# One 512-column matmul into a spare bank in the first up group, in place of six ahead of gate groups

## The chip, the core and the metric

The kernel runs on one core of a Trainium2 chip. The metric is the time of one execution on the device in microseconds, as the median of several runs; a profiled execution gives the rows shown here. The engines are named as in the profile: PE is TensorE's matmul row and PEld its weight loads, DVE is VectorE, ACT is ScalarE, POOL is GpSimd, and SP issues most of the DMAs.

## What is computed

One layer of an encoder on 256 positions of width 2048, in float32. Cut to what matters:

```
proj = rmsnorm(x, norm1_gain) @ w_in            # queries, keys and values of two groups of heads
o_d  = differential attention, 4 heads;  o_l = dilated windows, 8 heads
x    = x + concat(o_d, o_l) @ w_out
g, u = split(rmsnorm(x, norm2_gain) @ w_gate_up)  # 2 x 5632 columns
g    = depthwise_conv(g, conv_w, conv_b)          # width 3, over positions
x    = x + (silu(g) * u) @ w_down
out  = rmsnorm(x, final_gain)
```

## The kernel before

Each weight matrix is read from memory once, as 196 raw tiles of 128 x 2048 floats. Half a tile is a *unit*, and there are 392 of them, worked through in a fixed order that is written out by hand as a list (`add_unit`): 32 units for the values, 64 for queries and keys, 32 for the output projection, 176 for gate and up, 88 for the down projection.

To get near float32 accuracy, weights and activations are split into a high and a low part (`split`): ACT rounds a copy to the high part (line 121), and DVE subtracts it from the source to get the low part (line 122). A product is then three matmuls: high x high, high x low and low x high. `split_unit` does this for a unit three slots ahead of its use.

`products` (line 212) issues a unit's matmuls, all through `mm` (line 210 in the profile). There are two forms. In form A (values, output and down projection) a block of activations is the stationary operand and the weights move past it, 512 columns at a time; 12 matmuls make a unit. In form B (queries and keys, gate and up) a 128 x 128 block of weights is stationary and 256 positions of the activations move; 24 matmuls make a unit: eight on the high weights with the high activations, eight on the high weights with the low activations, eight on the low weights. In the profile the first 16 read whi and the last 8 read wlo.

In the gate and up stage there are 22 pairs. A pair is a gate group and then an up group, each of four units over k tiles 0-3, 4-7, 8-11 and 12-15, so 96 matmuls in a group and 192 in a pair. All four units of a group add into one accumulator of two banks (`acc`, two of them in turn). When a group is done, `gate` and `silu` or `gated` empty it on DVE and ACT. The pool `pat` has four more banks, handed out by `at_tile` (line 62): for scores, transposes, the broadcast of the token scale (line 150) just ahead of the first up group, and the last quarter of the down projection.

After the unit's own bookkeeping, and only in form B, a condition in `products` (line 236) picks out some units in which one more matmul is issued ahead of the 24. It takes the unit's first block of high weights as stationary operand, moves both parts of one k tile of the activations, 2 x 256 = 512 columns, and writes a bank of `pat` that nothing reads. Before the change the condition holds for the first unit of the gate groups of pairs 1, 5, 9, 13, 17 and 21:

```
            if U["first"] and U["key"][0] == "g" and U["key"][1] % 4 == 1:
                mm(at_tile(), wh[:, 0, :128], a[:, U["kts"][0]], True, True)
```

The order of instructions on every engine is that of the program (a manual schedule): the loop at the end loads raw tiles on SP's queue, splits the unit three slots ahead, issues the products of the present unit, and then the work that `at_slot` has put behind it.

Of the kernel before, what the change touches and what calls it, by code (L numbers as in the profile page):

```python
# [49 lines left out]
def encoder_layer(ctx, tc, xT_d, x_d, w_d, sm_d, tab_d, fg_d, id_d, oh_d, lnc_d, out_d):  # L50
# [11 lines left out]
    def at_tile():  # L62
        return pat.tile([128, 512], F32, name="at", tag="at")
# [145 lines left out]
    def mm(out, lhsT, rhs, start, stop):  # L209
        nc.tensor.matmul(out, lhsT, rhs, start=start, stop=stop)  # L210

    def products(s, ts=(0, 1)):
        U = units[s]
        if U["first"]:
            if U["key"] == ("d", 3):
                accs[U["key"]] = [at_tile(), at_tile()]
            else:
                P = acc.tile([128, 2, 512], F32, name="acc", tag="acc")
                accs[U["key"]] = P if U["form"] == "B" else [P[:, 0], P[:, 1]]
        P = accs[U["key"]]  # L220
        a = A[U["act"]]()
        hi, lo = W[s]
        nk = len(U["kts"])
        if U["form"] == "A":
            wh, wl = (w.rearrange("p (k c) -> p k c", k=2) for w in (hi, lo))
            for i, t in ((i, t) for i in range(2) for t in ts):
                kt = U["kts"][i]
                st, sp = U["first"] and i == 0, U["last"] and i == 1
                ah = a[:, kt, 0, t * 128:(t + 1) * 128]
                al = a[:, kt, 1, t * 128:(t + 1) * 128]  # L230
                mm(P[t], ah, wh[:, i], st, False)
                mm(P[t], ah, wl[:, i], False, False)
                mm(P[t], al, wh[:, i], False, sp)
        else:
            wh, wl = (w.rearrange("p (k c) -> p k c", k=4) for w in (hi, lo))
            if U["first"] and U["key"][0] == "g" and U["key"][1] % 4 == 1:

                mm(at_tile(), wh[:, 0, :128], a[:, U["kts"][0]], True, True)

            for j, (w, x_) in enumerate(((wh, 0), (wh, 1), (wl, 0))):  # L240
                for i, c in ((i, c) for i in range(nk) for c in range(2)):
                    mm(P[:, c, :S], w[:, i, c * 128:(c + 1) * 128], a[:, U["kts"][i], x_],
                       U["first"] and j == 0 and i == 0, U["last"] and j == 2 and i == nk - 1)
# [234 lines left out]
    for h in range(NH):  # L478
        g = 2 * h if h < 4 else h + 4
# [183 lines left out]
    for s in range(-AHEAD, NU):  # L663
        while n_loaded < NU // 2 and n_loaded * 2 <= s + AHEAD + 4:
            for _ in load_raw(n_loaded, 2 if n_loaded < 5 else 1):
                pass
            n_loaded += 1
            if X0 <= n_loaded < X0 + 4:
                load_x(n_loaded - X0)
        v = s + AHEAD  # L670
        if v < 8:
            split_unit(v, 2, lambda i: split_x(2 * v + i))
        elif v < NU:
            split_unit(v)
        if s == NU - AHEAD:
            break
        if s >= 0:
            products(s)
            del W[s]
            for f, a in post.pop(s, ()):  # L680
                f(*a)
    assert not post

    for t in range(2):
        for u in range(s, NU):
            products(u, (t,))
        final(t)
# [96 lines left out]
```

## Time and profile before

| what | value |
|---|---|
| median of 3 runs | 1137.55 us (1137.03 to 1138.54) |
| profiled execution, its own time | 1137.56 us |
| span of its instructions | 1135.8 us |
| TensorE matmul busy | 1123.0 us, 99% |
| TensorE weight load busy | 1043.9 us, 92% |
| VectorE busy | 677.6 us, 60% |
| ScalarE busy | 548.3 us, 48% |
| mean granted TensorE clock | 0.998 |

A row of the profile with two times gives the sum and the mean of one. Matmuls are pipelined, so the recorded duration of one is longer than the distance from its start to the next one's start. That distance is called the pitch here; it is taken from starts or from the length of a stretch by its count. The span is what lies between the first and the last instruction.

### The profile page before, as it was taken

Reading aid. Unit: us, or ns where it says so; the run is one execution under the profiler, and the core shown is the slowest. Engines: PE = TensorE matmul, PEld = TensorE weight load, DVE = VectorE, ACT = ScalarE, POOL = GpSimd, SP = SyncE. Lnnn points to the kernel's source line nnn. Section 1 sums busy time; section 2 is a strip of 40 time slices with the busy share of each in tenths; the row PEclk is TensorE's granted clock in tenths of the full one; section 3 lists DMA queues with packets and bytes.
Section 4 is the critical chain, followed back from the end, with each engine's and each line's share of the span. In section 5 each row is a group of like instructions: output and inputs, shape, how many; then the busy total and the mean of one; then the engine's idle time right before and its main releaser. Section 6 shows DMA issues by size and latency. Waiting matters only on the chain.

```text
span 1135.8 us, 18692 instructions
## 1 busy us (share of the span) xinstructions
PE 1123.0 (99%) x7930; PEld 1043.9 (92%) x7930; DVE 677.6 (60%) x841; ACT 548.3 (48%) x770; POOL 22.0 (2%) x40
## 2 busy tenths in 40 slices
PE   8999999999999999999999999999999999999996
PEld 6879999999988899999999999999999888888885
DVE  6844666766655575666666666656666545454543
ACT  7544456666555454544444454445444434343432
POOL 0000000001000000000000000000000000000000
PEclk9999999999999999999999999999999999999999
DMA  9568445445454546455555645454554655555552
GB/s 326 202 246 331 171 173 197 164 170 192 149 184 151 209 163 221 161 211 187 185 183 189 209 166 220 164 207 159 213 194 178 237 202 191 185 191 204 199 186 74
DMA packets 34092, 219.87 MB, mean 194 GB/s; under 512 B 3904, under 2 KB 4288, under 8 KB 9432
## 3 DMA queue, kind: packets, MB, share of 16 engines
q1 hardware_dynamic: 31536, 211.17, 52.0%
q0 software_dynamic: 1776, 6.69, 1.6%
q8 instruction: 62, 1.02, 0.3%
q10 hardware_dynamic: 696, 0.81, 0.2%
q14 instruction: 22, 0.18, 0.0%
HBM read 216.54 MB, written 5.27 MB: 195 GB/s over the span
## 4 chain that ended last, share of the span: by engine, by line
PE 95%; DMA 2%; DVE 1%; issue 1%; ACT 0%; POOLq 0%; POOL 0%; DVEq 0%; ACTq 0%
PE acc L210 87%; PE at L210 7%; DMA raw<-w 2%; DMA xT<-xT 1%; DVE wlo L122 1%; PE at L390 0%; DVE sqp L299 0%; PE at L455 0%; PE at L521 0%; ACT whi L121 0%; ACT jk L633 0%; POOLq L780 0%; PE at L251 0%; POOL r L639 0%; PE at L150 0%
## 5 line engine op out<-in xcount | busy, mean ns | idle before, releaser
L122 DVE TENSOR_TENSOR wlo<-raw,whi 128x1024 fp32r<-128x1024 f32 (+1 forms) x400 | 475.8, 1202 | 277.8 <-ACT whi L121 277.6
L121 ACT ACTIVATE whi<-raw 128x1024 fp32r<-128x1024 f32 (+1 forms) x400 | 408.9, 1036 | 282.3 <-PE acc L210 211.5
L210 PE MATMUL acc<-h2T,whi 128*128 128x256 f32 x2816 | 353.8, 278 | 0.0
L210 PEld LDWEIGHTS acc<-h2T,whi 128*128 128x128 f32 x2816 | 338.2, 188 | 0.4
L210 PE MATMUL acc<-h2T,wlo 128*128 128x256 f32 x1408 | 191.1, 278 | 0.0
L210 PEld LDWEIGHTS acc<-h2T,wlo 128*128 128x128 f32 x1408 | 175.2, 188 | 0.0
L210 PE MATMUL acc<-whi,aT 128*128 128x512 f32 x528 | 162.7, 389 | 0.0
L210 PE MATMUL acc<-hT,whi 128*128 128x256 f32 x1024 | 128.6, 278 | 0.0
L210 PEld LDWEIGHTS acc<-hT,whi 128*128 128x128 f32 x1024 | 121.7, 188 | 0.1
L210 PEld LDWEIGHTS acc<-whi,aT 128*128 128x128 f32 x528 | 99.1, 188 | 20.6
L210 PE MATMUL acc<-wlo,aT 128*128 128x512 f32 x264 | 102.7, 389 | 0.0
L210 PE MATMUL acc<-whi,hT 128*128 128x512 f32 x256 | 81.7, 396 | 2.1 <-ACT hT L124 2.1
L210 PE MATMUL acc<-whi,mT 128*128 128x512 f32 x256 | 82.7, 395 | 0.0
L210 PE MATMUL acc<-hT,wlo 128*128 128x256 f32 x512 | 68.7, 276 | 0.0
L210 PEld LDWEIGHTS acc<-hT,wlo 128*128 128x128 f32 x512 | 62.9, 188 | 0.0
L210 PEld LDWEIGHTS acc<-whi,hT 128*128 128x128 f32 x256 | 47.9, 188 | 15.1 <-ACT hT L124 3.9
L575 ACT ACTIVATE y<-gs,sm 128x256 f32<-128x256 f32 x44 | 24.1, 595 | 73.6 <-DVE gs L567 73.6
L210 PEld LDWEIGHTS acc<-wlo,aT 128*128 128x128 f32 x264 | 49.6, 188 | 10.2
L210 PEld LDWEIGHTS acc<-whi,mT 128*128 128x128 f32 x256 | 48.1, 188 | 9.7
L210 PE MATMUL at<-whi,aT 128*128 128x512 f32 x176 | 54.4, 389 | 0.0
L210 PE MATMUL acc<-wlo,hT 128*128 128x512 f32 x128 | 50.3, 393 | 0.0
L210 PE MATMUL acc<-wlo,mT 128*128 128x512 f32 x128 | 49.9, 390 | 0.0
(122 smaller groups left out, 620.9 us busy)
## 6 DMA issues: line engine op xcount, KB each, us to landing
raw<-w SPq DMA_DIRECT2D x191, 1024.0 KB, 4.9
raw<-w SPq DMA_DIRECT2D x8, 512.0 KB, 7.6
Z<-Td POOLq DMA_DIRECT2D x1, 3072.0 KB, 20.9
Xb<-Z POOLq DMA_DIRECT2D x12, 192.0 KB, 3.2
x<-x SPq DMA_DIRECT2D x4, 512.0 KB, 12.4
xT<-xT SPq DMA_DIRECT2D x7, 256.0 KB, 7.2
raw<-w SPq DMA_DIRECT2D x4, 256.0 KB, 5.4
fg<-fg POOLq DMA_DIRECT2D x1, 1024.0 KB, 4.9
```

The lines of the kernel that those rows point to most:

```text
L121: nc.scalar.activation(hi, src, AF.Copy)
L122: nc.vector.tensor_sub(lo, src, hi.bitcast(F32))
L210: nc.tensor.matmul(out, lhsT, rhs, start=start, stop=stop)
L575: nc.scalar.activation(y[:, c], gs[:, 1:S + 1], AF.Identity, bias=sm[:, C_CB + f:C_CB + f + 1], scale=w[1])
```

## The change

The condition is replaced. The extra matmul is now issued in one unit only: that of the first up group (pair 0) whose k tiles begin at 4, the second of its four units. The six ahead of gate groups are gone. All else is as it was.

```
-            if U["first"] and U["key"][0] == "g" and U["key"][1] % 4 == 1:
+            if U["key"] == ("u", 0) and U["kts"][0] == 4:
                 mm(at_tile(), wh[:, 0, :128], a[:, U["kts"][0]], True, True)
```

## Rows read from the trace of the kernel before

**Rows 1.** The page: busy time by engine (part 1), the chain that ended last by engine (part 4), and the two costliest groups of part 5 (line, engine, operation, tiles, count, then busy us and mean ns of one, then idle time before them).
```profile
PE 1123.0 (99%) x7930; PEld 1043.9 (92%) x7930; DVE 677.6 (60%) x841; ACT 548.3 (48%) x770; POOL 22.0 (2%) x40
...
PE 95%; DMA 2%; DVE 1%; issue 1%; ACT 0%; POOLq 0%; POOL 0%; DVEq 0%; ACTq 0%
...
L122 DVE TENSOR_TENSOR wlo<-raw,whi 128x1024 fp32r<-128x1024 f32 (+1 forms) x400 | 475.8, 1202 | 277.8 <-ACT whi L121 277.6
L121 ACT ACTIVATE whi<-raw 128x1024 fp32r<-128x1024 f32 (+1 forms) x400 | 408.9, 1036 | 282.3 <-PE acc L210 211.5
```

**Rows 2.** Waits of PE over the whole span: who waited for what, us in total, times, longest.
```profile
PE acc L210 <- ACT hT L124: 2.1, 2, 1.8
PE at L106 <- DVE warm L67: 1.2, 1, 1.2
```

**Rows 3.** Waits of all engines from 421 to 887 us, in the same columns; PE is in none of that list's lines as the one that waits.
```profile
ACT whi L121 <- PE acc L210: 68.1, 43, 1.8
```

**Rows 4.** The chain that ended last, in order of time, from 421 to 864 us: start us, us, what, and how many instructions.
```profile
421.23 0.23 PE at L210
421.46 87.05 PE acc L210 x768
508.52 0.23 PE at L210
508.74 90.45 PE acc L210 x768
599.20 0.23 PE at L210
599.43 87.04 PE acc L210 x768
686.47 0.23 PE at L210
686.70 90.45 PE acc L210 x768
777.15 0.23 PE at L210
777.38 87.04 PE acc L210 x768
864.42 0.23 PE at L210
```

**Rows 5.** Windows, each from the matmul after one of the six to the next of them (the last to the start of the down projection): stretch, us, then busy us and instructions of PE, PEld, DVE, ACT and POOL, granted clock, DMA share, GB/s. The counts take in the one or two matmuls that reach over an edge.
```profile
421.30:508.36 87.06, 87.06 (x770) 87.05 (x769) 55.87 (x64) 41.19 (x48) 0.00 (x0) 1.00 0.54 197
508.58:599.04 90.46, 90.46 (x770) 90.46 (x769) 55.87 (x64) 41.16 (x48) 0.00 (x0) 1.00 0.53 188
599.27:686.31 87.04, 87.04 (x770) 87.04 (x768) 55.89 (x64) 41.20 (x48) 0.00 (x0) 1.00 0.54 191
686.53:776.99 90.46, 90.46 (x770) 90.45 (x768) 55.88 (x64) 41.16 (x48) 0.00 (x0) 1.00 0.52 188
777.22:864.26 87.04, 87.04 (x769) 87.04 (x768) 55.89 (x64) 41.20 (x48) 0.00 (x0) 1.00 0.53 191
864.49:887.10 22.61, 22.61 (x193) 22.61 (x192) 13.95 (x16) 10.29 (x12) 0.00 (x0) 1.00 0.53 192
```

**Rows 6.** Groups of PE by line and shape from 430 to 500 us (busy us, mean ns of one, idle before).
```profile
L210 PE MATMUL acc<-h2T,whi 128*128 128x256 f32 x413 | 51.0, 276 | 0.0
```

**Rows 7.** The same from 520 to 590 us.
```profile
L210 PE MATMUL acc<-h2T,whi 128*128 128x256 f32 x400 | 51.2, 281 | 0.0
```

**Rows 8.** PE in order of time from 409 to 424.5 us: start us, us, what, count (neighbours of one kind are merged, and the length runs to the end of the last). The first up group begins at 409.58, the second gate group's extra matmul stands at 421.07.
```profile
409.33 0.59 PE L150 MATMUL at<-dg,ones 128*128 128x256 f32 x2
409.58 2.23 PE L210 MATMUL acc<-h2T,whi 128*128 128x256 f32 x16
411.65 1.10 PE L210 MATMUL acc<-h2T,wlo 128*128 128x256 f32 x8
412.59 2.05 PE L210 MATMUL acc<-h2T,whi 128*128 128x256 f32 x16
...
421.07 0.39 PE L210 MATMUL at<-h2T,whi 128*128 128x512 f32 x1
421.30 1.99 PE L210 MATMUL acc<-h2T,whi 128*128 128x256 f32 x16
...
424.04 0.73 PE L210 MATMUL acc<-h2T,whi 128*128 128x256 f32 x5
```

**Rows 9.** PE in order of time at the start of the down projection.
```profile
887.10 0.40 PE L210 MATMUL acc<-whi,aT 128*128 128x512 f32 x1
```

**Rows 10.** PE in order of time at the start of the down projection's last quarter, 3 x 22 x 12 = 792 matmuls later.
```profile
1066.64 0.39 PE L210 MATMUL at<-whi,aT 128*128 128x512 f32 x1
```

**Rows 11.** PE in order of time in the value stage, near the start of a stretch without other matmuls in it.
```profile
68.99 0.39 PE L210 MATMUL acc<-wlo,hT 128*128 128x512 f32 x1
```

**Rows 12.** The same at its end.
```profile
98.52 0.39 PE L210 MATMUL acc<-wlo,hT 128*128 128x512 f32 x1
```

**Rows 13.** The value stage's matmuls on the low weights from 68.9 to 98.7 us: count, duration ns min/median/max, first and last start.
```profile
L210 PE MATMUL acc<-wlo,hT x44: 392/392/392, 69.0 to 98.5; 128*128 128x512 f32 x44
```

**Rows 14.** Groups of PE by line and shape in the output projection, 366 to 379 us.
```profile
L210 PE MATMUL acc<-wlo,mT 128*128 128x512 f32 x20 | 7.8, 389 | 0.0
```

**Rows 15.** The same in the down projection, 900 to 1060 us.
```profile
L210 PE MATMUL acc<-wlo,aT 128*128 128x512 f32 x235 | 91.4, 389 | 0.0
```

## The prediction

> **What bounds the kernel.** I read the page's busy shares first. TensorE is busy for 99% of the span and no other engine is above 60% [rows 1]; the chain that ended last gives PE 95% [rows 1]. So only what shortens TensorE's own stream of instructions can shorten the run. The list of TensorE's waits says the same: the longest two groups are 2.1 and 1.2 us, for inputs of the first stage [rows 2]. From 421 us to the end of the gate and up groups TensorE waits for nobody, while ScalarE waits 68.1 us for TensorE to give weight buffers free [rows 3]. The weights are ready before they are wanted.
>
> Next comes the chain in order of time [rows 4]. It shows the six matmuls that the change takes out, 0.23 us each, and between them five stretches of 768 matmuls of one shape. They do not cost the same: 87.05, 90.45, 87.04, 90.45, 87.04 us. Per matmul that is 113.3 ns, then 117.8, and so on in turn: two **pitches**, a quick and a slow one, 4.44 ns apart, and the side changes at each of the six. What lies after the last of them fits: 864.49 to 887.10, 192 matmuls in 22.61 us, 117.8, slow [rows 5].
>
> What differs between quick and slow? Rows 5 set the stretches side by side: granted clock 1.00 (2.4 GHz, the higher level) in all, DMA share 0.52 to 0.54, VectorE 55.9 us and ScalarE 41.2 us of work in each. Weight loads fill each stretch as the matmuls do. The recorded duration carries a mark: 276 ns in a quick stretch [rows 6], 281 in a slow one [rows 7]. I take from this that the stream has two steady rhythms, that it stays in one until something of another length stands in it, and that one 512-column matmul among 256-column ones carries it across: slow to quick three times, quick to slow three times, no miss. I do not know what the rhythm is made of, and the sum does not need it.
>
> **The change, part by part.**
> Position. The new condition holds for one unit: the first up group's second. That group begins at 409.58 with 16 matmuls on whi and 8 on wlo for each unit, so the second unit begins at 412.59 [rows 8]. The new matmul stands there. It needs that unit's high weights and a bank. Nothing reads its result. The weights' split has run ahead (above) and the spare banks were last written by the broadcast of 409.33 [rows 8], so I put its wait at zero, between 0 and one whole split, 1.04 + 1.20 us [rows 1], which would show as idle time of PE. Neither queue of DMAs is touched.
>
> (a) Five matmuls fewer: 5 x 0.23 = 1.15 us less [rows 4]. They lie on the bounding stream, so all of it counts.
> (b) The rest of the first up group turns quick: from 412.59 to 421.07 there are 72 matmuls in 8.48 us, 117.8 ns, slow [rows 8]. 72 x 4.44 ns = 0.32 us less. The first matmuls behind a crossing are a little long: the 24 after the first of the six took from 421.30 to 424.04, 2.74 us against 24 x 113.3 = 2.72 [rows 8]; 0.02 us, paid three times before and once after, left out.
> (c) The second and fourth stretches turn quick: 2 x (90.46 - 87.05) = 6.82 us less [rows 5].
> (d) The last pair, 192 matmuls: 22.61 - 192 x 0.11334 = 0.85 us less [rows 5].
> (e) The three stretches that were quick stay quick: 0.
> (f) The down projection comes with 512 columns, from the quick side now and not the slow one. No row shows that entry. Its steady pitch before: 887.10 to 1066.64, 792 matmuls, 226.7 ns [rows 9, 10]. The one other steady pitch of this shape is the value stage's: from 68.99 to 98.52, where 44 matmuls on wlo are each third one, 43 x 3 = 129 steps, 228.9 ns [rows 11 to 13]. The bounds are 0 and 1,056 x 2.2 ns = 2.3 us more; no stretch is under 226.7, which excludes a gain. I take 0: the output projection, entered behind transposes, runs at 389 ns like the down projection [rows 14, 15], and the value stage at 392 throughout [rows 13], so the slower form goes with that stage and not with what came before it.
>
> Can the others follow a quicker TensorE? They did, for 87 us at a time, with VectorE at 64% and ScalarE at 47% of the stretch and no wait of PE [rows 2, 5]; next to be late would be the weights' DMA, at 0.54 in the quick stretches. The cover is wide. The tail behind the last matmul only moves forward.
>
> The sum: 1.15 + 0.32 + 6.82 + 0.85 = 9.14 us less. The profiled execution took 1137.56 us (span 1135.8 and 1.8 around it); the median of the runs is 1137.55, the same. 1137.56 - 9.14 = **1128.4 us**.
>
> **A rule against it.** Rows 5 give one shape two pitches, with nothing else different. The Trainium skill (TensorE: Matmul & The Clock Gate, section Back-to-back issue gap) gives a warm stream one gap by columns alone, N/2.4 + 2.5 ns, 109 ns at 256 and 216 at 512. By that rule a lone matmul has no after-effect, and the change would save five gaps, an estimate of 1.08 us, to 1136.5. The trace disagrees on the size (113.3 or 117.8) and on there being one value; the rival that it stands for is the second below.
>
> **Rivals.**
> 1. *The lone matmul does not cross there, and all stays slow.* Mid-group it stands ahead of a unit that adds to its sum, where the six stood ahead of a group's first unit, and the slow rhythm may be met at another point. Then the three quick stretches turn slow: 3 x 3.41 = 10.23 us more, 1.15 less, 1146.6 us: **slower**. For it: six cases are few, and only three go from slow to quick. Against it: from slow they went three times in three, the stream around the new place is the same 16 + 8 pattern of the same shapes, and 72 matmuls, three whole units, lie between it and the first of the six.
> It also prices a rhythm that does not last. With n quick matmuls after the crossing the change gives -1.15 + (2,304 - n) x 0.00444 us, where 2,304 is what was quick before and 4,104 what follows the new one (72 + 21 x 192). It is level with before at n = 2,045, some ten pairs; the longest quick stretch on record is 768, ended each time by one of the six and by nothing else. A fall back on the way lies anywhere between 1128.4 and 1146.6.
> 2. *The pitch belongs to the place and not to the matmul* (an alternation of pairs that the six only happen to stand at). Then only (a) is left: 1136.4 us, **no change** that can be told. Against it: the code of all pairs is the same, and the change of side comes in the very matmul at all six.
> 3. *The down projection takes the 228.9 ns form* when it is entered from the quick side: 1128.4 + 2.3 = 1130.7 us, still faster.
> 4. *The change does not do what it says*: the condition matching more than one unit, or none. Key and k tile together name one unit of 392; with none it would be rival 1 less 0.23 us. I give it no chance of its own.
>
> **How the numbers follow.** A measurement of this kernel can tell about 0.2%, 2.3 us, from no change. Forecast 0.78; rival 1 without any crossing 0.08; a fall back on the way 0.04, half of it faster and the rest split; rival 2 0.04; rival 3 0.06. Faster: 0.78 + 0.06 + 0.02 = 0.86; same: 0.04 + 0.01 = 0.05; slower: 0.08 + 0.01 = 0.09. The forecast's own range is the runs' scatter, 1137.03 to 1138.54 before, so 0.5 below and 1.0 above: 1127.9 to 1129.4. The range of 8 in 10 takes in rival 3 with half a microsecond on either side: 1127.4 to 1131.2, which holds 0.84.
>
> **What would show it.** Right: one row of at<-h2T,whi at 412.6 us; matmuls of 276 ns after it and 281 ahead of it; any window of 768 matmuls at 87.05 us; the down projection beginning at 887.1 - 9.1 = 878.0 us, at 226.7 ns and 389 ns. Rival 1: 281 ns to the end, the down projection at 896. Rival 2: 281 and 276 in turn with the old borders. Rival 3: 392 ns on aT. A wait of PE on whi or on a bank in the list of waits would show that (a) to (d) are paid for elsewhere. The forecast is wrong if the pitch after 413 us is not 113.3 ns for all of 4,104 matmuls.

## The result and the profile after

The changed kernel takes 1128.68 us (median of 4 runs, 1128.02 to 1129.09), the kernel before 1137.4 us beside it (4 runs, 1137.03 to 1138.54). The ratio is 0.9922, with a 95% interval of 0.991 to 0.9934: 0.8% faster. 1128.4 was forecast, with a range of 1127.4 to 1131.2. The profiled execution of after has a span of 1126.8 us, against 1135.8. One run of the kernel before, beside the experiments below, took 1242.82 us at a granted clock of 0.849, against 0.995 or more in all other runs, and is left out of every median here.

First the chain that ended last, in order of time from 400 us on (start us, us, what, how many). It answers to [rows 4].

```profile
409.74 0.43 PE at L150 x2
410.17 2.83 PE acc L210 x24
413.00 0.23 PE at L210
413.23 644.67 PE acc L210 x4896
```

The six are gone, and the one new matmul stands behind 24 of the first up group. What follows it is one piece up to the last quarter of the down projection: 4,104 matmuls of gate and up and 792 of the down projection. PE in order of time around it, which answers to [rows 8]:

```profile
409.82 2.23 PE L210 MATMUL acc<-h2T,whi 128*128 128x256 f32 x16
411.89 1.10 PE L210 MATMUL acc<-h2T,wlo 128*128 128x256 f32 x8
412.84 0.39 PE L210 MATMUL at<-h2T,whi 128*128 128x512 f32 x1
413.07 1.99 PE L210 MATMUL acc<-h2T,whi 128*128 128x256 f32 x16
414.89 1.07 PE L210 MATMUL acc<-h2T,wlo 128*128 128x256 f32 x8
415.80 1.41 PE L210 MATMUL acc<-h2T,whi 128*128 128x256 f32 x11
```

Ahead of it 8 matmuls on wlo take 412.84 - 411.89 = 0.95 us, behind it 415.80 - 414.89 = 0.91 us. That the pitch stays so is to be seen in windows of 768 matmuls, at the start and at the end of the stage. The columns are those of [rows 5]:

```profile
413.30:500.34 87.04, 87.04 (x770) 87.04 (x769) 56.34 (x65) 42.59 (x50) 0.00 (x0) 1.00 0.55 194
790.34:877.38 87.04, 87.04 (x770) 87.04 (x769) 55.92 (x64) 41.19 (x48) 0.00 (x0) 1.00 0.54 193
```

The matmuls on the stage's high and low weights from 425 us on (count, duration ns min/median/max, first and last start) have the 276 ns of [rows 6] to the last, and the 281 of [rows 7] is gone:

```profile
L210 PE MATMUL acc<-h2T,whi x2665: 276/276/276, 424.8 to 877.2; 128*128 128x256 f32 x191
L210 PE MATMUL acc<-h2T,wlo x1336: 276/276/276, 425.8 to 878.1; 128*128 128x256 f32 x191
```

The down projection in order of time at its start, then at its last quarter, and its groups from 900 to 1050 us, which answer to [rows 9, 10, 15]:

```profile
878.20 0.39 PE L210 MATMUL acc<-whi,aT 128*128 128x512 f32 x1
```

```profile
1057.73 0.39 PE L210 MATMUL at<-whi,aT 128*128 128x512 f32 x1
```

```profile
L210 PE MATMUL acc<-wlo,aT 128*128 128x512 f32 x221 | 86.0, 389 | 0.0
```

792 matmuls in 179.53 us, 226.7 ns, as before. Last the waits (in total, times, longest): ScalarE's for TensorE in the gate and up stage, 412 to 878 us, then PE's own over the whole span. They answer to [rows 3] and [rows 2].

```profile
ACT whi L121 <- PE acc L210: 64.1, 43, 1.6
```

```profile
PE acc L210 <- ACT hT L124: 1.8, 1, 1.8
PE at L106 <- DVE warm L67: 1.2, 1, 1.2
```

The quicker stream brought no new wait of PE, and ScalarE still waits for it.

### The profile page after: what moved, and what is told of

The parts are those of the page before. It is cut to its first block, busy times and chain, and to the rows that moved or that the text cites. A ratio compares the mean times of both kernels' runs of the same rounds, so it can differ in the third digit from the quotient of the medians.

```text
span 1126.8 us, 18682 instructions
## 1 busy us (share of the span) xinstructions
PE 1114.8 (99%) x7925; PEld 1036.7 (92%) x7925; DVE 677.8 (60%) x841; ACT 548.4 (49%) x770; POOL 22.0 (2%) x40
## 4 chain that ended last, share of the span: by engine, by line
PE 98%; DMA 0%; issue 0%; ACT 0%; DVE 0%; POOLq 0%; POOL 0%; DVEq 0%
PE acc L210 90%; PE at L210 7%; PE at L390 0%; DMA sm<-sm 0%; PE at L521 0%; PE at L455 0%; ACT jk L633 0%; POOLq L780 0%; PE at L251 0%; POOL r L639 0%; PE at L150 0%; DVEq L780 0%; ACT hT L124 0%; DVE x L645 0%; DVE x L631 0%
## 5 line engine op out<-in xcount | busy, mean ns | idle before, releaser
L210 PE MATMUL acc<-h2T,whi 128*128 128x256 f32 x2816 | 348.4, 276 | 0.0
L210 PEld LDWEIGHTS acc<-h2T,whi 128*128 128x128 f32 x2816 | 332.8, 188 | 0.2
L210 PE MATMUL acc<-h2T,wlo 128*128 128x256 f32 x1408 | 188.4, 276 | 0.0
L210 PEld LDWEIGHTS acc<-h2T,wlo 128*128 128x128 f32 x1408 | 172.8, 188 | 0.0
```

## The experiments

My theory: the stream of 256-column matmuls has two steady rhythms, and one matmul of another length can carry it from one to the other. The rivals: the pitch goes with the place, or with the absence of the six; something else about the lone matmul (its bank, its weights loaded twice) does it; and the crossing depends on the point in the slow rhythm at which it comes, which was the mechanism of the prediction's first rival. The kernels ran in three groups, each on one chip; the kernel before took 1137.24, 1137.48 and 1137.45 us there (13 runs, 6 and 1). All diffs are against the changed kernel.

**No extra matmul at all.**

```
-            if U["key"] == ("u", 0) and U["kts"][0] == 4:
-                mm(at_tile(), wh[:, 0, :128], a[:, U["kts"][0]], True, True)
```

> No extra matmul at all. Two rhythms, crossed by the lone matmul: the slow rhythm of the first gate group stays to the down projection, 281 ns matmuls throughout; against the changed kernel 4,104 x 4.44 ns = 18.2 us more and 0.23 less, 1146.7 us. Rival, that the six matmuls ahead of gate groups were themselves what disturbed the stream and the quick pitch is what is left without them: 276 ns throughout and 1128.4 us.

Measured: 1146.12 us (4 runs, ratio to the kernel before 1.0076, 1.0059 to 1.0093). The chain in order of time:

```profile
409.46 0.43 PE at L150 x2
409.90 665.70 PE acc L210 x4920
```

With the 179.5 us of the down projection's 792 matmuls taken off, 4,128 matmuls take 486.2 us: 117.8 ns. Without a lone matmul the slow rhythm in which the up group begins lasts to the end of the stage. The six did not disturb a quick stream; three of them made the quick stretches.

**A second one, ahead of gate group 11.**

```
-            if U["key"] == ("u", 0) and U["kts"][0] == 4:
+            if (U["key"] == ("u", 0) and U["kts"][0] == 4) or (U["key"] == ("g", 11) and U["first"]):
```

> The changed kernel with one more such matmul ahead of gate group 11. Two rhythms: quick to that matmul, slow after it, on 11 pairs x 192 = 2,112 matmuls; 0.23 + 2,112 x 4.44 ns = 9.6 us above the changed kernel, 1138.3 us, and the change of side lies at the new matmul, a place where neither kernel had one. Rival, that the pitch belongs to the place: only 0.23 us more, 1128.9 us.

Measured: 1137.74 us (ratio to before 1.0002, 0.9993 to 1.0012), some 0.6 us under the expectation; the broadcast ahead of the up group stands 0.7 us earlier in this execution (409.05) than in that of the changed kernel (409.74). The chain, its count of 2,904 being 2,112 of this stage and 792 of the next:

```profile
409.05 0.43 PE at L150 x2
...
412.31 0.23 PE at L210
412.54 225.77 PE acc L210 x1992
638.31 0.23 PE at L210
638.53 428.29 PE acc L210 x2904
```

113.3 ns up to the new matmul; then (428.29 - 179.5) / 2,112 = 117.8 ns. The side changes at a place where neither kernel had a matmul. The pitch does not belong to the place.

**256 columns in place of 512.**

```
-                mm(at_tile(), wh[:, 0, :128], a[:, U["kts"][0]], True, True)
+                mm(at_tile()[:, :S], wh[:, 0, :128], a[:, U["kts"][0], 0], True, True)
```

> The lone matmul has 256 columns, as long as its neighbours; same place, same weights, same spare bank. If it is the odd length that carries the stream across: no crossing, 281 ns to the down projection, 4,104 x 4.44 ns = 18.2 us more and 0.12 less than the changed kernel, 1146.8 us. If it is the write to another bank, or the weights loaded twice in a row: a crossing as before and 1128.6 us.

Measured: 1146.4 us (one run). PE in order of time around it, then the stage's matmuls from 425 us on:

```profile
412.45 0.28 PE L210 MATMUL at<-h2T,whi 128*128 128x256 f32 x1
...
414.45 1.11 PE L210 MATMUL acc<-h2T,wlo 128*128 128x256 f32 x8
```

```profile
L210 PE MATMUL acc<-h2T,whi x2604: 281/281/281, 424.8 to 885.0; 128*128 128x256 f32 x186
```

The bank and the double weights alone do nothing here. It is the length; that the 512 columns also take in the low part of the activations was not tried apart from it.

**128 columns.**

```
-                mm(at_tile(), wh[:, 0, :128], a[:, U["kts"][0]], True, True)
+                mm(at_tile()[:, :128], wh[:, 0, :128], a[:, U["kts"][0], 0, :128], True, True)
```

> The lone matmul has 128 columns, half as long as its neighbours. If any odd length crosses: quick after it, 276 ns, 1128.6 us. If only a longer one does: slow to the down projection, 1146.8 us. I cannot tell which; the first crossings of the query stage follow transposes of 128 columns sometimes and sometimes not.

Measured: 1146.19 us (one run), slow throughout:

```profile
412.26 0.22 PE L210 MATMUL at<-h2T,whi 128*128 128x128 f32 x1
...
414.26 1.11 PE L210 MATMUL acc<-h2T,wlo 128*128 128x256 f32 x8
```

From the lone one to the first on wlo, 17 matmuls, 414.26 - 412.26 = 2.00 us; with 256 columns it was 414.45 - 412.45 = 2.00 us. What the shorter matmul saved was given back within the next 16, to 0.01 us, and the rhythm was not left. That is one point of the slow rhythm and one run; a 128-column matmul elsewhere was not tried.

**Two of 512 columns in a row.**

```
-                mm(at_tile(), wh[:, 0, :128], a[:, U["kts"][0]], True, True)
+                for _ in range(2):
+                    mm(at_tile(), wh[:, 0, :128], a[:, U["kts"][0]], True, True)
```

> Two 512-column matmuls in a row at the same place. If each one crosses: back in the slow rhythm, 18.2 + 0.23 us above the changed kernel, 1147.1 us. If the first crosses and the second is only one more step of a settled stream: quick, 1128.9 us.

Measured: 1128.15 us (one run). The chain:

```profile
412.28 0.47 PE at L210 x2
412.74 644.67 PE acc L210 x4896
```

Quick, in the same 644.67 us as after one. So "each one crosses" is too simple: from quick a lone one leads to slow, but the second of a pair, behind one that has just left the slow side, does not.

**One, two and three matmuls later in the unit.** The condition moves into the inner loop; (0, 0, 1), (0, 1, 0) and (0, 1, 1) put the matmul behind the first, second and third of the unit's 24.

```
-            if U["key"] == ("u", 0) and U["kts"][0] == 4:
-                mm(at_tile(), wh[:, 0, :128], a[:, U["kts"][0]], True, True)
...
                 for i, c in ((i, c) for i in range(nk) for c in range(2)):
+                    if U["key"] == ("u", 0) and U["kts"][0] == 4 and (j, i, c) == (0, 0, 1):
+                        mm(at_tile(), wh[:, 0, :128], a[:, U["kts"][0]], True, True)
```

> The 512-column matmul stands one matmul later, behind the first of the unit's 24 instead of ahead of it. All crossings so far stood at the start of a unit, and a unit is 24 matmuls, so all of them came at the same count in threes of the slow stream. If the crossing does not depend on where in the slow rhythm it comes: quick, 1128.7 us. If it does, this one may fail: slow, 1146.9 us.

> The 512-column matmul stands two matmuls later, behind the second of the unit's 24. As for one later: 1128.7 us if a crossing comes at any point of the slow rhythm, 1146.9 us if this point fails.

> The 512-column matmul behind the third of the unit's 24. Two matmuls later failed, none and one later crossed. If the slow rhythm repeats every three matmuls and the point in the three decides, this is the same point as the changed kernel's: quick, 1128.3 us. If the place in the unit decides and only its first two crossed: slow, 1147 us.

Measured: 1128.25, **1147.23** and 1127.83 us (one run each). PE in order of time behind the lone matmul, one later:

```profile
414.51 1.07 PE L210 MATMUL acc<-h2T,wlo 128*128 128x256 f32 x8
415.42 1.75 PE L210 MATMUL acc<-h2T,whi 128*128 128x256 f32 x14
```

Two later:

```profile
415.30 1.10 PE L210 MATMUL acc<-h2T,wlo 128*128 128x256 f32 x8
416.24 1.93 PE L210 MATMUL acc<-h2T,whi 128*128 128x256 f32 x15
```

Three later:

```profile
414.09 1.07 PE L210 MATMUL acc<-h2T,wlo 128*128 128x256 f32 x8
415.00 1.98 PE L210 MATMUL acc<-h2T,whi 128*128 128x256 f32 x16
```

Compare the eight on wlo: 0.91, 0.94 and 0.91 us. The same instruction, moved by a single matmul to either side, gives the whole gain or costs 19 us more.

**Two later in the next unit.** The same edit with `U["kts"][0] == 8` and (0, 1, 0).

> The 512-column matmul behind the second of the 24 in the next unit of the same group, 24 matmuls on from the one that failed; 24 is eight threes. If the point in the three decides: slow again, 1147 us. If the failure was a chance of that one execution or of that unit: quick, 1128.5 us.

Measured: 1146.07 us (one run), slow again behind the lone matmul:

```profile
416.97 1.10 PE L210 MATMUL acc<-h2T,wlo 128*128 128x256 f32 x8
417.92 1.34 PE L210 MATMUL acc<-h2T,whi 128*128 128x256 f32 x10
```

Counted from the start of the group's second unit, 0, 1 and 3 matmuls on cross, and 2 and 24 + 2 do not. With 24 a multiple of three, all five agree with one point in three at which the slow rhythm is not left. The weight loads, shown with the last experiment below, confirm it.

**One unit earlier, ahead of the up group's first unit.**

```
-            if U["key"] == ("u", 0) and U["kts"][0] == 4:
+            if U["key"] == ("u", 0) and U["first"]:
```

> The matmul stands ahead of the first unit of the same up group, 24 matmuls earlier, just behind the broadcast of the token scale. If it crosses there as well: 24 x 4.44 ns = 0.1 us below the changed kernel, 1128.6 us, which no timing tells from it, but the trace shows 276 ns from 410 us on. If the broadcast's own two matmuls ahead of it hold the stream in the slow rhythm: slow throughout, 1146.9 us.

Measured: 1128.32 us (4 runs, ratio to before 0.9917, 0.9899 to 0.9935). It crosses there too:

```profile
409.68 0.24 PE at L210
409.91 647.39 PE acc L210 x4920
```

(647.39 - 179.5) / 4,128 = 113.3 ns. This is 0.4 us under the changed kernel, within the scatter of that one's runs: no better version that a measurement could tell.

**In gate group 0, ahead of its third unit, and none in the up group.**

```
-            if U["key"] == ("u", 0) and U["kts"][0] == 4:
+            if U["key"] == ("g", 0) and U["kts"][0] == 8:
```

> The 512-column matmul ahead of the third unit of gate group 0, and none in the up group; the broadcast of the token scale, two 256-column matmuls of another kind, then stands in the quick rhythm. If the quick rhythm outlives it: quick from 404 us on, (48 + 24) x 4.44 ns = 0.3 us below the changed kernel, 1128.0 us. If the broadcast puts the stream back in the slow rhythm: 1146.6 us.

Measured: 1146.52 us (one run). The time is that of the second answer, but the trace shows another reason:

```profile
405.66 1.11 PE L210 MATMUL acc<-h2T,wlo 128*128 128x256 f32 x8
406.61 2.05 PE L210 MATMUL acc<-h2T,whi 128*128 128x256 f32 x16
```

The eight on wlo take 406.61 - 405.66 = 0.95 us: it did not cross in the first place. The weight loads, one for each matmul on a row of their own (PEld), tell why. In the slow rhythm each third load takes 192 ns and the other two 187 or 188: 255 of the 765 recorded from 508.8 to 598.9 us in the kernel before, always three apart. In the quick rhythm none is above 188. Loads of the kernel before, slow from 510 and quick from 425 us on (count, duration ns min/median/max, first and last start us):

```profile
L210 PEld LDWEIGHTS acc<-h2T,whi x500: 187/188/192, 509.9 to 597.9; 128*128 128x128 f32 x167
L210 PEld LDWEIGHTS acc<-h2T,whi x472: 187/188/188, 424.8 to 504.5; 128*128 128x128 f32 x158
```

So the lone matmul's own load shows at which point of the three it stands. First the six of the kernel before, then the changed kernel, one later and three later:

```profile
L210 PEld LDWEIGHTS at<-h2T,whi x6: 187/188/188, 421.0 to 864.2; 128*128 128x128 f32 x6
L210 PEld LDWEIGHTS at<-h2T,whi x1: 188/188/188, 412.7 to 412.7; 128*128 128x128 f32 x1
L210 PEld LDWEIGHTS at<-h2T,whi x1: 188/188/188, 412.5 to 412.5; 128*128 128x128 f32 x1
L210 PEld LDWEIGHTS at<-h2T,whi x1: 188/188/188, 412.3 to 412.3; 128*128 128x128 f32 x1
```

Then two later, two later in the next unit, and this one in gate group 0:

```profile
L210 PEld LDWEIGHTS at<-h2T,whi x1: 192/192/192, 413.3 to 413.3; 128*128 128x128 f32 x1
L210 PEld LDWEIGHTS at<-h2T,whi x1: 192/192/192, 415.0 to 415.0; 128*128 128x128 f32 x1
L210 PEld LDWEIGHTS at<-h2T,whi x1: 192/192/192, 403.4 to 403.4; 128*128 128x128 f32 x1
```

The three 512-column matmuls that did not cross are those whose own load is the long one of the three. In the changed kernel and three matmuls later the long load is the one just ahead of it, one matmul later the second ahead. Ahead of the up group's first unit, right behind the broadcast, the lone matmul's load takes 188 ns as well. The 256- and the 128-column matmul, with 188 ns too and the long load just ahead, stood at the point of the changed kernel, so it was not their point that kept them from crossing. Why that one point fails stays open, and so does whether the quick rhythm outlives the broadcast.

## Why the prediction was right

- **Position and waits.** As put: one matmul behind the 24th of the first up group, at 412.84. The first up group began 0.24 us later than in the profiled execution of before (409.82 against 409.58), ahead of anything that the change touches. No wait of PE came with it.
- **(a)** Five matmuls fewer at 0.23 us: the one left takes 0.23 us in the chain.
- **(b) to (e)** The 4,104 matmuls behind it take 644.67 - 179.5 = 465.1 us, 113.3 ns, to the end of the stage. Measured from the start of the first up group to the start of the down projection, before took 887.10 - 409.58 = 477.52 us and after 878.20 - 409.82 = 468.38: 9.14 us less, which is the sum. The spans differ by 9.0, since the later start of 0.24 us takes a part back, and the medians by 8.7; the runs of either kernel scatter by 1 us or more.
- **(f)** 389 ns and 226.7 ns from the quick side. The slower form of the value stage did not appear, so rival 3 is out. The down projection has the same pitch entered from the slow side (before) and from the quick one (after).
- **Rival 1** fell for the changed kernel, but its mechanism is real. "The slow rhythm may be met at another point" is what happens two matmuls later: 1147.23 and 1146.07 us, near the 1146.6 that the rival gave. What decided the case was the reason that the prediction named last: 72 matmuls, three whole units, lie between the new place and the first of the six, so the new one met the slow rhythm at the same point of its three. The trace bears it out: in both kernels the load just ahead of the lone one's is the long one (192 ns, begun at 420.8 us in before and at 412.6 in after). That the crossing "went three times in three" told less than it seemed. All three stood at starts of units, but not, as the expectation for one matmul later has it, at the same count in threes: for the third and fifth of the six the long load is the second ahead (598.7 and 776.6 us). Two of the three points were on record and the one that fails was not, and the prediction knew of no three. The new place was safe by its 72 matmuls, not by the count of crossings.
- **Rival 2** is refuted by the crossing ahead of gate group 11, at a place that had none. The same stream, at a granted clock of 1.00, ran at 113.3 or at 117.8 ns per matmul by what stood thousands of matmuls ahead of it. The formula of the Trainium skill that was weighed (TensorE: Matmul & The Clock Gate, section Back-to-back issue gap) has one gap by columns alone. The section calls it the isolated gap, and lets both operations set the spacing in a stream of weight loads and matmuls in pairs. This stream is of such pairs, and no single spacing fits it.

What the rhythms are made of was not found. The runs show what a crossing from the slow one depends on (length and point of the lone matmul), not the part of the chip that keeps the rhythm. From quick to slow, one was tried only at starts of units, three in the kernel before and the one ahead of gate group 11, each a multiple of 24 matmuls behind the last crossing; all four crossed.

## What to carry to other kernels

Where one engine is busy for 99% of the span, compare the pitch of equal stretches before looking for waits: here 4% lay between two stretches of the same code, at the same clock, with no wait in either. Where such a stream has two pitches, one instruction of another length can be worth far more than its own time; put it once, early, and look in the trace which side the stream is on behind it. Check its place by moving it: a gain that rests on the count of instructions ahead of it can be lost by a single one more, so it has to be looked at again after every edit upstream.

## What was not expected of the hardware

The point of crossing repeats every three matmuls: 0, 1 and 3 later gave 1128 us, 2 and 26 later 1146 to 1147. The slow rhythm carries a mark of it: each third weight load takes 192 ns in place of 187 or 188, and a 512-column matmul whose own load is the long one does not cross. A 128-column matmul among 256-column ones cost as much as one of 256 columns (2.00 us for it and the 16 behind it, in both cases; one run each). And two 512-column matmuls in a row cross once, not twice: 644.67 us for the 4,896 matmuls behind them, as behind one.
